# The low parts of weights split by GpSimd: a subtraction replaced by a negation on ScalarE and an accumulating DMA

## The chip, the cores and the metric

The kernel runs on one core of one Trainium2 chip. The core has TensorE (matrix products into PSUM), VectorE, ScalarE, GpSimd, a queue called SP that issues DMAs, and 16 DMA engines. The metric is the device time of one execution in microseconds. The profile shows one execution; its rows carry short names: PE is TensorE, PEld its weight load, DVE VectorE, ACT ScalarE, POOL GpSimd.

## The reference, cut to what matters

Two layers of a decoder trunk over 512 tokens of width 1024, in 32-bit floats. Each layer has a wide input projection, three token mixers (a sparse one "A", a dilated one "B", a windowed one "C"), sigmoid gates, an output projection and an MLP.

```
for l in range(DEPTH):                       # DEPTH = 2
    u = rmsnorm(h, attn_norm[l])
    (aq, ak, av, iq, ik, iw, bq, bk, bv, cq, ck, cv, gates) = split_columns(u @ w_in[l])
    ...                                      # mixers A, B, C
    g = sigmoid(gates.reshape(Bsz, L, 3, D_MODEL))
    merged = g[:,:,0]*(o_a @ w_a[l]) + g[:,:,1]*(o_b @ w_b[l]) + g[:,:,2]*(o_c @ w_c[l])
    h = h + merged @ w_o[l]
    u = rmsnorm(h, mlp_norm[l])
    h = h + square(relu(u @ w_up[l])) @ w_down[l]
return rmsnorm(h, final_norm)
```

## The kernel before, in words

TensorE multiplies in a reduced 32-bit format (`F32R`). To keep the accuracy, every operand is held as two tiles: `hi`, its rounded value, and `lo`, what the rounding left. Each product is then three matmuls (`mm3`: hi with hi, hi with lo, lo with hi).

Weights come in tiles of 128 partitions and up to 1024 columns, two steps of the inner dimension side by side. `load` issues the DMAs from SP into a `raw` tile (line 261; 6 buffers), lets ScalarE copy it into `hi` (line 264; 5 buffers), and forms `lo = raw - hi` (line 265; 5 buffers). The subtraction runs on VectorE, or, where the caller says so, on GpSimd. `load_chunk` makes the four tiles of a projection's eight inner steps; its `pool_tiles` names those of the four that GpSimd splits:

- all four tiles of each of the eight gate chunks of a layer (`gates`), 64 in all, of 768 columns;
- the last tile of the six chunks of a layer's dilated projections (`b_project`), 12 in all, of 768 columns;
- a few tiles of the index, narrow and sparse projections (`idx_project`, `small_project`, `a_project`): five of 1024 columns and two of 656.

That makes 83. The chunks of the output projection, the branches, and the MLP are split by VectorE alone.

The order of the work is set when the program is built. `merge` and `pipeline` interleave attention, gates and projections in program order; a scheduler then gives each engine, at each step, the earliest piece of work that by its reckoning is ready. Only in the first stretch is the order of SP, ScalarE and VectorE written by hand. On the chip each engine runs its queue strictly in order, and each wait holds what stands behind it. A projection of 128 tokens runs eight inner steps in one PSUM bank, the last tile of a chunk being needed from the seventh step on. After it, its result is turned on VectorE (`rope`, lines 321 to 329) and transposed on TensorE (line 337).

Of the kernel before, what the change touches and what calls it, by code (L numbers as in the profile page):

```python
# [20 lines left out]
ALU = mybir.AluOpType  # L21
# [19 lines left out]
def f32(ap):  # L41
    return ap.bitcast(F32)

class Trunk:
# [211 lines left out]
    def load(self, parts, width, lo_eng=None):  # L256

        nc = self.nc
        raw = self.st([P, 1024], "raw")
        for dst, src in parts:  # L260
            nc.sync.dma_start(dst(raw), src)
        hi = self.st([P, 1024], "hi", F32R)
        lo = self.st([P, 1024], "lo", F32R)
        nc.scalar.copy(hi[:, :width], raw[:, :width])  # L264
        (lo_eng or nc.vector).tensor_tensor(lo[:, :width], raw[:, :width], f32(hi[:, :width]), op=ALU.subtract)  # L265
        return hi, lo

    def load_chunk(self, w, k0, nk, cols, pool_tiles=()):
# [878 lines left out]
def build(tr):  # L1147
# [7 lines left out]
    with tr.tc.manual_schedule(engines={ET.SP, ET.Activation, ET.DVE}):  # L1155
# [16 lines left out]
        next(steps[1])  # L1172
        angle(2)
        wk = load(0, (0,))
        xload(2)
        next(steps[1])
        angle(1)
        next(steps[1])
        wk += load(2)
        xload(3)  # L1180
        next(steps[2])
        wk += load(4, (0,))
        next(steps[2])
        next(steps[3])
# [118 lines left out]
```

## Time and profile before

| | |
|---|---|
| median of 3 runs | 1762.99 us (1761.1 to 1763.85) |
| profiled execution, its time | 1759.4 us |
| span of its instructions | 1757.7 us |
| TensorE busy | 1690.6 us, 96% |
| VectorE busy | 1273.6 us, 72% |
| ScalarE busy | 917.7 us, 52% |
| GpSimd busy | 187.3 us, 11% |
| subtractions to lo on GpSimd | 83, 158.8 us |

Busy time is the union of an engine's instructions. It says how full an engine is, and not yet whether it sets the end. What a stretch waits for is read from the idle time ahead of TensorE's instructions and from what released them.

### The profile page before, as it was taken

How to read it: one execution, taken by the hardware profiler on the slowest of the kernel's cores; microseconds unless marked ns; L12 is line 12 of the kernel's file. 1: busy time of each engine (PE TensorE's matmuls, PEld its weight loads, DVE VectorE, ACT ScalarE, POOL GpSimd, SP SyncE). 2: the span in 40 equal slices, each digit the busy share in tenths (PEclk: the TensorE clock that was granted, in tenths of full speed). 3: DMA queues.
4: the chain of work that ended last, by engine and by line, in shares of the span. 5: the costliest groups of instructions: out<-in, count | busy, mean ns of one | idle time of the engine just before them, and what ended most of it. 6: DMA issues, size and time to landing. Idle time of an engine off the chain costs nothing.

```text
span 1757.7 us, 24534 instructions
## 1 busy us (share of the span) xinstructions
PE 1690.6 (96%) x8640; PEld 1429.0 (81%) x8640; DVE 1273.6 (72%) x2560; ACT 917.7 (52%) x1861; POOL 187.3 (11%) x163
## 2 busy tenths in 40 slices
PE   7989999999989999999999999999999999999997
PEld 5779899777779888888887798988777798888886
DVE  7986858766855868685988757596677568585858
ACT  5575645537423645454545856465473255445454
POOL 3310211221000000000012113021110000000000
PEclk9999999999999999999999999999999999999999
DMA  6224343332663142423343243433236523232412
GB/s 198 67 74 130 79 109 81 106 77 81 205 210 97 61 132 86 142 89 104 108 118 72 61 132 90 117 98 82 63 115 215 204 81 100 96 116 76 144 48 72
DMA packets 202908, 190.54 MB, mean 108 GB/s; under 512 B 17824, under 2 KB 159136, under 8 KB 202784
## 3 DMA queue, kind: packets, MB, share of 16 engines
q1 hardware_dynamic: 202784, 188.97, 36.3%
q8 instruction: 68, 1.11, 0.3%
q14 instruction: 56, 0.46, 0.1%
HBM read 167.91 MB, written 18.87 MB: 106 GB/s over the span
## 4 chain that ended last, share of the span: by engine, by line
PE 74%; DVE 16%; ACT 3%; DMA 3%; issue 3%; POOL 1%; SPq 0%; POOLq 0%; DVEq 0%; ACTq 0%
PE psg L288 19%; PE psg L290 19%; PE psg L289 18%; DMA sg<-sgd 2%; PE psl L288 2%; PE psl L289 2%; PE psl L290 2%; DVE a L682 1%; PE pst L290 1%; PE pst L289 1%; PE pst L288 1%; PE pst L337 1%; DVE t L325 1%; PE psl L369 1%; DVE lo L926 1%
## 5 line engine op out<-in xcount | busy, mean ns | idle before, releaser
L288 PE MATMUL psg<-uT,hi 128*128 128x512 f32 (+1 forms) x896 | 346.7, 387 | 0.0
L290 PE MATMUL psg<-uT,lo 128*128 128x512 f32 (+1 forms) x896 | 344.5, 384 | 0.0
L289 PE MATMUL psg<-uT,hi 128*128 128x512 f32 (+1 forms) x896 | 344.3, 384 | 0.0
L264 ACT CAST hi<-raw 128x768 fp32r<-128x768 f32 (+4 forms) x256 | 228.9, 899 | 154.9 <-PE psg L289 68.8
L265 DVE TENSOR_TENSOR lo<-raw,hi 128x1024 fp32r<-128x1024 f32 (+4 forms) x173 | 190.6, 1105 | 58.4 <-ACT hi L264 56.9
L289 PE MATMUL psg<-lo,uT 128*128 128x384 f32 (+2 forms) x624 | 218.8, 351 | 3.5 <-DVE lo L265 2.4
L265 POOL TENSOR_TENSOR lo<-raw,hi 128x768 fp32r<-128x768 f32 (+2 forms) x83 | 158.8, 1926 | 584.5 <-ACT hi L264 549.9
L288 PE MATMUL psg<-hi,uT 128*128 128x384 f32 (+2 forms) x624 | 220.6, 355 | 0.2 <-ACT uT L240 0.2
L290 PE MATMUL psg<-hi,uT 128*128 128x384 f32 (+2 forms) x624 | 218.6, 350 | 0.0
L290 PEld LDWEIGHTS psg<-uT,lo 128*128 128x128 f32 x896 | 168.8, 188 | 31.0
L289 PEld LDWEIGHTS psg<-uT,hi 128*128 128x128 f32 x896 | 169.1, 189 | 29.2 <-issue 0.7
L288 PEld LDWEIGHTS psg<-uT,hi 128*128 128x128 f32 x896 | 169.0, 189 | 29.1 <-issue 0.7
L289 PEld LDWEIGHTS psg<-lo,uT 128*128 128x128 f32 x624 | 117.7, 189 | 11.7 <-DVE lo L265 3.4
L925 ACT CAST hi<-raw 128x1024 fp32r<-128x1024 f32 x80 | 84.2, 1052 | 81.5 <-DVE raw L1000 34.3
L288 PEld LDWEIGHTS psg<-hi,uT 128*128 128x128 f32 x624 | 117.7, 189 | 7.2 <-ACT uT L240 0.6
L290 PEld LDWEIGHTS psg<-hi,uT 128*128 128x128 f32 x624 | 117.5, 188 | 6.7
L208 POOL TENSOR_TENSOR st<-st,mhalf 128x1 f32<-128x1 f32 x20 | 16.2, 811 | 946.3 <-DVE st L206 941.9
L926 DVE TENSOR_TENSOR lo<-raw,hi 128x1024 fp32r<-128x1024 f32 x80 | 96.0, 1218 | 25.4 <-ACT hi L925 25.4
L288 PE MATMUL psg<-hi,a 128*128 128x512 f32 x288 | 112.7, 391 | 0.2
L956 DVE TENSOR_TENSOR a<-t,a 128x512 fp32r<-128x512 f32 (+1 forms) x128 | 78.9, 620 | 46.9 <-ACT a L955 45.3
L290 PE MATMUL psg<-hi,a 128*128 128x512 f32 x288 | 112.4, 390 | 0.0
L289 PE MATMUL psg<-lo,a 128*128 128x512 f32 x288 | 112.1, 389 | 0.0
(230 smaller groups left out, 3348.2 us busy)
## 6 DMA issues: line engine op xcount, KB each, us to landing
raw<-in_w_in_dram SPq DMA_DIRECT2D x336, 128.0 KB, 2.8
raw<-in_w_up_dram SPq DMA_DIRECT2D x128, 256.0 KB, 3.8
raw<-in_w_down_dram SPq DMA_DIRECT2D x48, 512.0 KB, 4.9
raw<-in_w_in_dram SPq DMA_DIRECT2D x24, 512.0 KB, 3.7
sgd<-sg SPq DMA_DIRECT2D x48, 256.0 KB, 2.6
sg<-sgd SPq DMA_DIRECT2D x48, 256.0 KB, 3.9
raw<-in_w_o_dram SPq DMA_DIRECT2D x16, 512.0 KB, 3.8
a<-in_w_down_dram SPq DMA_DIRECT2D x16, 512.0 KB, 4.3
```

The costliest lines, as they stand in the source:

```text
L264: nc.scalar.copy(hi[:, :width], raw[:, :width])
L265: (lo_eng or nc.vector).tensor_tensor(lo[:, :width], raw[:, :width], f32(hi[:, :width]), op=ALU.subtract)
L288: nc.tensor.matmul(out, lh, rh, start=start, stop=False, **kw)
L289: nc.tensor.matmul(out, lh, rl, start=False, stop=False, **kw)
L290: nc.tensor.matmul(out, ll, rh, start=False, stop=stop, **kw)
L325: self.last_dve = nc.vector.tensor_tensor(v1, v1, v2, op=ALU.add)
L337: self.nc.tensor.transpose(ps[:, i, :], src[:, i * P : (i + 1) * P], self.ident)
L369: nc.tensor.matmul(out, q, k[:, 0, c0 : c0 + n], start=True, stop=False)
L682: nc.vector.tensor_tensor(lo[at], x[own], f32(dst[own]), op=ALU.subtract)
L925: nc.scalar.copy(hi, x)
L926: nc.vector.tensor_tensor(lo, x, f32(hi), op=ALU.subtract)
L956: v.tensor_tensor(lo, x, f32(hi), op=ALU.subtract)
```

## The change

Where GpSimd was given the split, ScalarE now writes `lo = -hi` after its copy to `hi`, and GpSimd's queue issues a DMA that adds the raw tile to `lo` in place. Where VectorE makes the split, all stays as it was.

```
         nc.scalar.copy(hi[:, :width], raw[:, :width])
-        (lo_eng or nc.vector).tensor_tensor(lo[:, :width], raw[:, :width], f32(hi[:, :width]), op=ALU.subtract)
+        if lo_eng is None:
+            nc.vector.tensor_tensor(lo[:, :width], raw[:, :width], f32(hi[:, :width]), op=ALU.subtract)
+        else:
+            nc.scalar.mul(lo[:, :width], f32(hi[:, :width]), -1.0)
+            lo_eng.dma_start(lo[:, :width], raw[:, :width], accum_op=ALU.add)
         return hi, lo
```

## Rows read from the trace of the kernel before

**Rows 1.** The page's busy times: us, share of the span, instructions.

```profile
PE 1690.6 (96%) x8640; PEld 1429.0 (81%) x8640; DVE 1273.6 (72%) x2560; ACT 917.7 (52%) x1861; POOL 187.3 (11%) x163
```

**Rows 2.** The chain that ended last: shares of the span by engine.

```profile
PE 74%; DVE 16%; ACT 3%; DMA 3%; issue 3%; POOL 1%; SPq 0%; POOLq 0%; DVEq 0%; ACTq 0%
```

**Rows 3.** Groups by form: busy us, mean ns of one, then idle time before.

```profile
L265 POOL TENSOR_TENSOR lo<-raw,hi 128x768 fp32r<-128x768 f32 x76 | 142.9, 1894 | 515.2 <-ACT hi L264 480.5 <-DMA raw<-in_w_in_dram 16.6 <-DVE a L682 11.6
...
L264 ACT CAST hi<-raw 128x1024 fp32r<-128x1024 f32 x104 | 109.3, 1051 | 86.8 <-PE psl L290 27.0 <-PE psg L289 22.0 <-DMA raw<-in_w_up_dram 14.8
L264 ACT CAST hi<-raw 128x768 fp32r<-128x768 f32 x112 | 92.3, 835 | 19.6 <-PE psg L290 7.0 <-PE psg L289 6.8 <-ACT a L672 2.3
```

**Rows 4.** Waits of TensorE and ScalarE: us in total, times, longest.

```profile
PE pst L337 <- DVE t L325: 13.5, 10, 3.3
...
PE pst L337 <- DVE t L219: 10.8, 2, 9.0
PE pst L757 <- ACT a L750: 3.3, 6, 0.7
...
PE psg L289 <- DVE lo L265: 2.4, 2, 1.2
...
PE pst L337 <- DVE st L197: 1.6, 1, 1.6
PE pst L337 <- DVE t L526: 1.6, 2, 0.8
...
ACT hi L264 <- DMA raw<-in_w_in_dram: 4.8, 3, 3.9
```

**Rows 5.** Order of time, VectorE and GpSimd: start us, us, what, count.

```profile
81.35 7.08 DVE L493 SCALAR_TENSOR_TENSOR a<-t,iw,a 128x384 f32<-128x384 f32 x4
...
91.09 0.61 DVE L493 SCALAR_TENSOR_TENSOR a<-t,iw,a 128x384 f32<-128x384 f32 x1
...
81.92 8.17 POOL L265 TENSOR_TENSOR lo<-raw,hi 128x768 fp32r<-128x768 f32 x4 [18.01 <-ACT hi L264]
```

**Rows 6.** Busy times from 88 to 95 us, granted clock, DMA share, GB/s.

```profile
88.00:95.00 7.00, 3.69 (x18) 3.48 (x18) 6.83 (x13) 2.86 (x7) 2.09 (x2) 0.76 0.64 142
```

**Rows 7.** Order of time, first and last of 12 dilated chunks: split, first use.

```profile
149.62 1.85 POOL L265 TENSOR_TENSOR lo<-raw,hi 128x768 fp32r<-128x768 f32 x1 [27.47 <-ACT hi L264]
...
153.36 0.33 PE L289 MATMUL psg<-lo,uT 128*128 128x384 f32 x1
...
1155.09 1.84 POOL L265 TENSOR_TENSOR lo<-raw,hi 128x768 fp32r<-128x768 f32 x1 [16.59 <-ACT hi L264]
...
1159.42 0.34 PE L289 MATMUL psg<-lo,uT 128*128 128x384 f32 x1
```

**Rows 8.** Order of time, TensorE: transposes in a new chunk's first block.

```profile
188.10 0.52 PE L337 MATMUL pst<-ident,t 128*128 128x128 f32 x3 [0.96 <-DVE t L325]
```

**Rows 9.** Order of time, first gate behind the dilated projections.

```profile
200.35 0.84 ACT L264 CAST hi<-raw 128x768 fp32r<-128x768 f32 x1 [0.58 <-ACT a L672]
...
209.30 0.39 PE L290 MATMUL psg<-uT,lo 128*128 128x512 f32 x1
```

**Rows 10.** Order of time, start: first split by GpSimd and its first use.

```profile
10.65 2.36 POOL L265 TENSOR_TENSOR lo<-raw,hi 128x1024 fp32r<-128x1024 f32 x1 [1.59 <-ACT hi L264]
...
13.07 0.79 PE L289 MATMUL psg<-lo,uT 128*128 128x512 f32 x1 [1.17 <-POOL lo L265]
```

**Rows 11.** Order of time, sparse projection, last tile: split and first use.

```profile
359.53 4.23 POOL L265 TENSOR_TENSOR lo<-raw,hi 128x1024 fp32r<-128x1024 f32 x2 [23.16 <-ACT hi L264]
...
362.79 0.39 PE L289 MATMUL psg<-lo,uT 128*128 128x512 f32 x1
```

**Rows 12.** DMA issues: count, KB each, median us from issue to landing.

```profile
raw<-in_w_up_dram SPq DMA_DIRECT2D x128, 256.0 KB, 3.8
...
a<-t SPq DMA_DIRECT2D x16, 128.0 KB, 2.9
...
raw<-in_w_down_dram SPq DMA_DIRECT2D x48, 512.0 KB, 4.9
```

## What was predicted, before the change was run

> **What bounds the kernel now.** I read the page's busy times first: TensorE is at work for 1690.6 of 1757.7 us, 96% [rows 1]. The chain of work that ended last agrees: TensorE holds 74% of it, VectorE 16%, ScalarE 3%, GpSimd 1% [rows 2]. So nothing is won by GpSimd being quicker in itself. A change can only act on the 67 us in which TensorE stands still, or add to them. What the reader should look for is therefore who ends TensorE's waits, and how long before TensorE wants it each low part is there.
>
> The groups by form price the operations: GpSimd's subtraction takes 1.89 us for a tile of 768 columns (76 times); five more tiles have 1024 columns (2.36 us [rows 10]) and two 656. ScalarE's copy from raw to hi takes 0.84 and 1.05 us for the same tiles [rows 3]. The list of TensorE's waits is led by VectorE [rows 4]. One stretch shows why: four updates by L493 take 7.08 us together, while the next one takes 0.61 [rows 5]. GpSimd is subtracting four tiles just then. The instructions that are stretched in this way, beside GpSimd's subtraction alone, read on-chip memory only (L493, L325, L219, L265, a copy in L526). Only what TensorE waits for counts.
>
> **What goes.** The 83 GpSimd subtractions go, and with them the blocking. Of TensorE's waits, L325 ends 13.5 us; two of these, of 1.0 us each, had no blocked instruction ahead (one is shown, 0.96 us [rows 8]), which leaves 11.6. L219 ends 10.8, of which 9.0 is the start of the program, so 1.8. L197 ends 1.6 (behind a blocked L219), L526 1.6, and VectorE's own split L265 2.4 [rows 4]. That is 19.0 us. The longest of these waits, 3.31 us, is followed by a stretch of 7 us with a mean granted clock of 0.76, about 3.4 us at 1.2 GHz in place of 2.4, which lost 1.7 us [rows 6]. Together 20.7; a blocked instruction is not always the whole of the wait behind it, so I take **20 us back**. The bounds are 0 (descriptor writing by GpSimd blocks as much as its reading did) and 21.
>
> **What ScalarE gets.** A negation reads and writes tiles of the same form as the copy ahead of it, so it costs the same: 76 x 0.84 + 5 x 1.05 + 2 x 0.72 (the last by its columns) = 71 us more, 52% to 56% of the span. Behind each stands whatever is queued on ScalarE: casts of projected queries and keys, exponentials, the next hi. TensorE waits for ScalarE directly very little (exponentials: 3.3 us in 6 waits [rows 4]), and VectorE, which waits for it, is idle 28% of the time. ScalarE's 3% of the chain, and a little of VectorE's 16% that stands behind ScalarE, make 7% of 71: **+5 us**. Bounds 0 and 71.
>
> **What the accumulating DMA costs.** Its landing L, from the end of the negation until lo may be read, stands in place of the subtraction. No row shows such a DMA. The nearest are: on-chip to on-chip, 128 KB, 2.9 us; weight loads of 256 KB 3.8 and of 512 KB 4.9 [rows 12]. The tile has 384 KB. As a plain copy between the tiles of on-chip memory that is about 3.0, the low end. An accumulation reads 768 KB; the two loads rise by 1.1 us per 256 KB, so 6.0 is the high end. I take the middle, **L = 4.5**, as the sources are on chip, but twice the bytes are read and the weight loads share the engines.
>
> The Trainium skill, "DMA: Bandwidth & Descriptors", section on the anatomy of one DMA on the GpSimd path, gives a fit of 2.0 us plus bytes over 436e3, which would be 2.9 us here (an estimate by that page); my sum would then come to -10. "Collectives: The Full Stack", on the bandwidth ceiling, says that a reducing transfer needs two source reads and runs at half the rate; by both pages an estimate is 3.8 us, and the sum comes to -2. No row here shows either.
>
> Against the subtraction, lo of a 768-column tile comes later by 0.84 + L - 1.84 = L - 1.0, that is 3.5 us. Where that is more than the slack, TensorE waits:
>
> - Last tile of each of 12 chunks of the dilated projections: in the first chunk GpSimd is done at 151.47 and the first product that needs the tile starts at 153.36, slack 1.9; in the last chunk the slack is 2.5 [rows 7]. The twelve have 1.3 to 2.5, mean 1.77, so they come L - 2.77 = 1.7 late, 21 us in all. The schedule can put other ready work there: three transposes of the block before already stand in the middle of a new chunk, behind five of its eight steps [rows 8]. I count half: **10.4**.
> - The first gate behind a pair of dilated projections (4 times): hi starts at 200.35, and more copies follow. Copy and negation three times are 5.0 us, with 0.5 for casts between; the third lo lands at 205.9 + 4.5 = 210.4, and is wanted at 209.30 [rows 9]. 4 x 1.1 = **4.4**.
> - Start: GpSimd began at 10.65, when hi was done; negation to 11.7, landing at 16.2; wanted at 13.07 already [rows 10]. **3.1**.
> - Projection of the sparse attention, 1024 columns: begun at 359.53, done 2.36 later at 361.9, wanted at 362.79 [rows 11]. Later by 1.05 + 4.5 - 2.36 = 3.2, so 2.3 too late, in both layers: **4.6**.
> - The other tiles have 2.4 us or more, most of them 4 to 30; what lateness is left there is under 1 us each, taken as nothing.
>
> GpSimd's queue holds little behind the DMA: powers of one column, most of them far from these tiles. SP's loads wait longer for a raw tile to come free, since the DMA reads it last. That costs nothing: a weight tile's landing ended a wait of ScalarE's copy only 3 times, 4.8 us, from the projection weights [rows 4]. If this cover were gone, each of the 83 would be late by the same 3.5 us.
>
> Sum: 10.4 + 4.4 + 3.1 + 4.6 = 22.5 late, + 5 on ScalarE, - 20 given back = **+8 us**. The profiled execution took 1759.4 us (a span of 1757.7 and 1.7 around it), so 1767; the median of the runs is 3.6 above it, so **1771**. A measurement of this kernel tells about 0.2%, 3.5 us, from no change.
>
> **Rivals.**
> - *Short landing, faster.* At L = 3.0 the chunks lose 2, the gates 0, the start 1.6, the sparse projection 1.6: 5.2 + 5 - 20 = -10, 1753. It decides from L below about 3.9 on. For it: the 2.9 of the on-chip copy [rows 12]. Against: that one is a third of the size and reads once. By the fit of "DMA: Bandwidth & Descriptors" this is the case that would come.
> - *Cancelling, no change.* With L near 3.9 the two sides meet and the time stays at 1763. For it: 3.8 us, the row of 256 KB [rows 12]. Against: the two sides have nothing to do with each other, and the band is only 0.5 us of L wide. By the half rate of "Collectives: The Full Stack" this one would come.
> - *Long landing that nothing fills.* L = 6.0 and no other work in the gaps: 39 + 10.4 + 4.6 + 7.6 = 62, + 5 - 20 = +47, 1810. For it: TensorE's order is fixed, and a wait of 1.2 us for VectorE's split, twice, stands unfilled today [rows 4]. Against: the transposes of rows 8.
> - *No relief, or ScalarE on the path.* If GpSimd's descriptor work blocks VectorE as its reads did, +28, 1791; if a third of the 71 us lands on the path, some +27, 1790. For it: VectorE waits for ScalarE in many places. Against: ScalarE has 44% left.
>
> **How the numbers follow.** Forecast, slower by 4 to 25 us (1767 to 1788): 0.37. Short landing: 0.30. Cancelling: 0.13. Long and unfilled: 0.14. No relief or ScalarE: 0.06. So faster 0.30, same 0.13, slower 0.57. The range goes from a little beyond the short landing to the long one, 1751 to 1808; signs differ within it, so the forecast's own range stands above.
>
> **What would show it.** Right: L493, L325 and L219 at their unblocked 0.6 to 0.75 us everywhere; no subtraction on GpSimd; a new ScalarE group of 83 at 0.8 to 1.05 us; a median landing of 4 to 5 us; TensorE's waits now ended by the DMA into lo, about 20 us in all, at the last tile of the chunks above all. Wrong: a landing under 3.9 with waits gone (faster), or waits for lo of 3 us and more, perhaps with the clock falling to 1.2 GHz behind them, as it did behind the 3.31 us wait (slower than the range).

## The result, and the profile after

The kernel became slower by 3.1%: a median of 1815.12 us (1814.39 to 1822.07, 4 runs) beside 1762.05 us for the kernel before on the same chip, ratio 1.031 with an interval of 1.0282 to 1.0337. That is 53 us where +8 was forecast, 7 us above the top of the range. The sign was right, the size was not.

The page's busy times of the kernel after, to be set beside [rows 1]:

```profile
span 1812.7 us, 24736 instructions
...
PE 1709.8 (94%) x8640; PEld 1438.8 (79%) x8640; DVE 1239.8 (68%) x2560; ACT 978.8 (54%) x1944; POOL 100.7 (6%) x163
```

The span grew by 55.0 us. TensorE does the same 8640 products, so there are only two places for it: TensorE's time without work went from 67.1 us (1757.7 less 1690.6) to 102.9, which is +35.8, and its busy time rose by 19.2. Two thirds of the loss are waiting, one third is the same work done more slowly.

The chain that ended last, shares of the span by engine, answers to [rows 2]:

```profile
PE 60%; issue 14%; DMA 11%; DVE 8%; ACT 5%; SPq 0%; POOL 0%; POOLq 0%; ACTq 0%; DVEq 0%
```

VectorE's share went from 16% to 8%, and the DMAs' from 3% to 11%. The fall of TensorE's share to 60% is not to be read as idleness: the chain here runs back through GpSimd's issues, and seven pieces of "issue" ahead of such issues, of 18 to 24 us each, make 149 us, in which TensorE is busy for 140. Who ends the waits is in the waits of TensorE, in total, times and longest, to be set beside [rows 4]:

```profile
PE psg L293 <- DMA lo<-raw: 42.7, 17, 6.9
PE psg L294 <- DMA lo<-raw: 19.0, 14, 2.7
PE psg L292 <- DVE sg L895: 10.0, 9, 3.6
PE pst L341 <- DVE t L219: 9.0, 1, 9.0
PE pst L341 <- DVE t L329: 2.3, 4, 0.9
```

The diff moved the lines below it down by four (L289 is L293, L290 is L294, L325 is L329, L337 is L341). The waits for `rope` fell from 13.5 us to 2.3 and VectorE's split no longer ends one in L293: the relief came. (Not all of that fall need be relief. Where TensorE does not stand for `lo`, in e3 below, the waits for `rope` are 9.8 us and those for VectorE's split 2.0; some of them may be over here because TensorE comes later.) The accumulating DMA now ends 31 waits of 61.7 us together, where the prediction counted 22.5. L293 multiplies the projections' weights, L294 the gates'.

That VectorE is free shows in the order of time at the place of [rows 5], the same four updates of 384 columns:

```profile
84.88 2.72 DVE L497 SCALAR_TENSOR_TENSOR a<-t,iw,a 128x384 f32<-128x384 f32 x4
```

They took 7.08 us beside GpSimd's subtraction, and 2.72 now, though GpSimd issued one of its DMAs in the midst of them, from 86.19 to 87.06 us. So this issue did not block them. The Trainium skill, "SBUF — State Buffer", section "Who interferes with whom", has it that a VectorE instruction with two inputs in on-chip memory contends with GpSimd where GpSimd reads that memory, and not where it only writes. The trace agrees with the first half (7.08 us beside a subtraction, which reads); that an issue only writes is shown by no run.

The new operations, groups by form (busy us, mean ns of one, idle before), ScalarE's two and GpSimd's one:

```profile
L268 ACT ACTIVATE lo<-hi 128x768 fp32r<-128x768 f32 x76 | 64.0, 845 | 1.4
L268 ACT ACTIVATE lo<-hi 128x1024 fp32r<-128x1024 f32 x5 | 5.3, 1056 | 0.1
...
L269 POOL DMA_DIRECT2D lo<-raw x83 | 71.8, 869 | 730.1 <-ACT lo L268 281.7 <-DMA raw<-in_w_in_dram 175.9 <-DVE m L513 47.8
```

And the landings, KB each and median us from issue to landing:

```profile
raw<-in_w_up_dram SPq DMA_DIRECT2D x128, 256.0 KB, 3.9
lo<-raw POOLq DMA_DIRECT2D x76, 384.0 KB, 4.8
...
lo<-raw POOLq DMA_DIRECT2D x5, 512.0 KB, 6.7
```

The negation costs what the copy costs, 0.85 us. The landing of 384 KB was taken at 4.5 and is 4.8 in the median; the weight loads that priced it [rows 12] are where they were.

One dilated chunk in the order of time (ScalarE's negation, GpSimd's issue, TensorE's wait), the one of [rows 7]:

```profile
148.46 0.85 ACT L268 ACTIVATE lo<-hi 128x768 fp32r<-128x768 f32 x1
...
149.60 0.86 POOL L269 DMA_DIRECT2D lo<-raw  x1 [22.81 <-ACT lo L268]
...
152.12 0.34 PE L292 MATMUL psg<-hi,uT 128*128 128x384 f32 x1
155.23 0.44 PE L293 MATMUL psg<-lo,uT 128*128 128x384 f32 x1 [2.77 <-DMA lo<-raw]
```

From the end of the negation (149.31) to the first product with `lo` 5.92 us pass. TensorE does the six steps whose tiles are there and the first product of the seventh, and then nothing for 2.77 us: no transpose and no product of another chunk steps in. In eight of the twelve chunks it is so; in the other four the three transposes of [rows 8] stand ahead of the wait, and 1.0 to 2.3 us of waiting are left. Read in this way, the twelve chunks have 4.2 to 6.1 us from negation to use, 5.05 in the mean, and each of them waits, 1.04 to 2.86 us, 23.8 together. The other long waits are 6.87 at the start, 3.84 at the index projection of the second layer, 3.51 and 3.35 at the sparse projections. The start, the gate behind the dilated projections and the first sparse projection in the order of time, to be set beside [rows 9 to 11]:

```profile
10.61 1.06 ACT L268 ACTIVATE lo<-hi 128x1024 fp32r<-128x1024 f32 x1
...
19.86 0.79 PE L293 MATMUL psg<-lo,uT 128*128 128x512 f32 x1 [6.87 <-DMA lo<-raw]
...
213.97 1.58 ACT L268 ACTIVATE lo<-hi 128x768 fp32r<-128x768 f32 x2
...
220.65 0.50 PE L294 MATMUL psg<-uT,lo 128*128 128x512 f32 x1 [2.68 <-DMA lo<-raw]
...
383.78 1.06 ACT L268 ACTIVATE lo<-hi 128x1024 fp32r<-128x1024 f32 x1
...
390.77 0.50 PE L293 MATMUL psg<-lo,uT 128*128 128x512 f32 x1 [3.51 <-DMA lo<-raw]
```

From negation to use these are 8.2, 5.8 (the gate's is the first of the two negations, over at 214.82) and 5.9 us.

The rest is clock. Busy times by stretch (PE, PEld, DVE, ACT, POOL, then granted clock, DMA share, GB/s), three of ten stretches at 1.2 GHz in place of 2.4:

```profile
156.40:159.80 3.40, 3.40 (x12) 3.40 (x12) 0.29 (x1) 0.64 (x2) 0.00 (x0) 0.50 0.60 153
...
391.90:395.30 3.40, 3.40 (x10) 2.62 (x9) 2.14 (x5) 0.21 (x1) 0.00 (x0) 0.50 0.86 199
...
1282.80:1289.60 6.80, 5.55 (x13) 4.40 (x14) 2.14 (x5) 0.21 (x1) 0.00 (x0) 0.50 0.84 184
sum 37.40, PE 35.58 PEld 31.05 DVE 16.74 ACT 8.49 POOL 1.42; mean PE 3.56 PEld 3.10 DVE 1.67 ACT 0.85 POOL 0.14
```

All ten begin during or within 2 us behind a wait for `lo` of 1.85 to 3.84 us. Three waits of 2.2 to 2.8 us (at 1049.6, 1070.1 and 1182.9) have none behind them, so not every wait is followed by one. TensorE is busy for 35.6 us in them, half of which, 17.8, is lost. The kernel before had two such stretches with 9.1 us of work, 4.6 lost. That is 13.2 of the 19.2 us by which busy time rose; where the other 6.0 come from is open.

### The profile page after: what moved, and what is told of

It is laid out like the page before. It is cut to its first block, busy times and chain, and to the rows that moved or that the text cites. A ratio compares the mean times of both kernels' runs of the same rounds, so it can differ in the third digit from the quotient of the medians.

```text
span 1812.7 us, 24736 instructions
## 1 busy us (share of the span) xinstructions
PE 1709.8 (94%) x8640; PEld 1438.8 (79%) x8640; DVE 1239.8 (68%) x2560; ACT 978.8 (54%) x1944; POOL 100.7 (6%) x163
## 4 chain that ended last, share of the span: by engine, by line
PE 60%; issue 14%; DMA 11%; DVE 8%; ACT 5%; SPq 0%; POOL 0%; POOLq 0%; ACTq 0%; DVEq 0%
PE psg L293 16%; PE psg L294 15%; PE psg L292 15%; DMA lo<-raw 7%; DMA sg<-sgd 2%; PE psl L293 2%; PE psl L294 2%; PE psl L292 2%; DMA raw<-in_w_in_dram 2%; ACT hi L264 1%; PE pst L341 1%; PE pst L293 1%; PE pst L294 1%; PE pst L292 1%; ACT a L390 1%
## 5 line engine op out<-in xcount | busy, mean ns | idle before, releaser
L294 PE MATMUL psg<-uT,lo 128*128 128x512 f32 (+1 forms) x896 | 347.6, 388 | 19.1 <-DMA lo<-raw 19.0
L293 PE MATMUL psg<-uT,hi 128*128 128x512 f32 (+1 forms) x896 | 345.3, 385 | 0.0
L264 ACT CAST hi<-raw 128x768 fp32r<-128x768 f32 (+4 forms) x256 | 229.3, 898 | 141.3 <-PE psg L293 63.3
L293 PE MATMUL psg<-lo,uT 128*128 128x384 f32 (+2 forms) x624 | 226.5, 363 | 42.7 <-DMA lo<-raw 42.7
L292 PE MATMUL psg<-hi,uT 128*128 128x384 f32 (+2 forms) x624 | 224.2, 363 | 1.5 <-ACT uT L240 1.2
L294 PE MATMUL psg<-hi,uT 128*128 128x384 f32 (+2 forms) x624 | 224.2, 360 | 0.0
L266 DVE TENSOR_TENSOR lo<-raw,hi 128x1024 fp32r<-128x1024 f32 (+4 forms) x173 | 183.5, 1064 | 58.5 <-ACT hi L264 55.7
L294 PEld LDWEIGHTS psg<-uT,lo 128*128 128x128 f32 x896 | 169.2, 189 | 57.0 <-DMA lo<-raw 26.2
L293 PEld LDWEIGHTS psg<-uT,hi 128*128 128x128 f32 x896 | 169.6, 189 | 29.4 <-issue 0.7
L293 PEld LDWEIGHTS psg<-lo,uT 128*128 128x128 f32 x624 | 121.5, 195 | 56.2 <-DMA lo<-raw 48.4
L292 PEld LDWEIGHTS psg<-hi,uT 128*128 128x128 f32 x624 | 121.1, 194 | 9.5 <-ACT uT L240 1.6
L294 PEld LDWEIGHTS psg<-hi,uT 128*128 128x128 f32 x624 | 121.8, 195 | 7.4 <-DVE uT L241 0.4
L269 POOL DMA_DIRECT2D lo<-raw x83 | 71.8, 869 | 730.1 <-ACT lo L268 281.7
L294 PE MATMUL psg<-hi,a 128*128 128x512 f32 x288 | 112.3, 390 | 0.0
L293 PE MATMUL psg<-lo,a 128*128 128x512 f32 x288 | 112.1, 389 | 0.0
L411 DVE TENSOR_TENSOR a<-pst,a 128x384 fp32r<-128x384 f32 (+1 forms) x100 | 60.4, 623 | 70.2 <-ACT a L410 69.6
```

Source lines behind the costliest of these rows:

```text
L266: nc.vector.tensor_tensor(lo[:, :width], raw[:, :width], f32(hi[:, :width]), op=ALU.subtract)
L269: lo_eng.dma_start(lo[:, :width], raw[:, :width], accum_op=ALU.add)
L292: nc.tensor.matmul(out, lh, rh, start=start, stop=False, **kw)
L293: nc.tensor.matmul(out, lh, rl, start=False, stop=False, **kw)
L294: nc.tensor.matmul(out, ll, rh, start=False, stop=stop, **kw)
L411: self.last_dve = nc.vector.tensor_tensor(pt[:, 1, :n], ps, f32(pt[:, 0, :n]), op=ALU.subtract)
```

## The experiments

Theory, formed on this profile: the relief is as large as forecast or larger; the loss is lateness of `lo` at a few places in TensorE's fixed order, which nothing fills, plus the clock behind these waits. Rivals: the DMAs cost by their traffic whoever reads them; ScalarE's 71 us are on the path; the 64 gate transfers crowd the queue and so make the others late. All ratios are to the kernel before on the same chip, with their intervals.

| kernel | median us (runs) | ratio | TensorE's waits for the DMA into lo |
|---|---|---|---|
| changed kernel | 1815.12 (4) | 1.031 [1.0282, 1.0337] | 61.7 us, 31 |
| e2: no low part made | 1726.13 (4) | 0.983 [0.9813, 0.9847] | none |
| e1: negation alone | 1737.15 (4) | 0.9883 [0.9866, 0.9901] | none |
| e3: low part made, not read | 1749.32 (5) | 0.9955 [0.9939, 0.997] | none |
| e4: DMA for gates, GpSimd for projections | 1762.0 (10) | 1.0025 [1.0015, 1.0035] | 19.5, 15 |
| e5: DMA for projections, GpSimd for gates | 1817.11 (4) | 1.0333 [1.0314, 1.0351] | 45.9, 17 |
| e12: DMA for 12 dilated tiles, VectorE for the rest | 1781.65 (4) | 1.014 [1.0118, 1.0162] | 25.5, 12 |
| e13: DMA for gates, VectorE for the rest | 1761.45 (10) | 1.0023 [1.0009, 1.0037] | 18.6, 15 |
| e9: plain copy in place of the accumulation | 1778.19 (4) | 1.0118 [1.0093, 1.0143] | 30.7, 21 |
| e7: first tile of a chunk in place of the last | 1779.47 (4) | 1.0123 [1.0102, 1.0144] | 30.6, 18 |
| e10: DMA for first tiles alone, VectorE for the rest | 1760.47 (10) | 1.001 [1.0001, 1.0019] | 2.6, 1 |
| e6: VectorE for all 83 | 1744.87 (4) | 0.9927 [0.9907, 0.9946] | none |
| e11: e6, and 83 copies off the core | 1748.15 (5) | 0.9947 [0.9932, 0.9962] | none |

One reservation holds for all but e9: the scheduler that writes the engines' queues answers to each edit with another order on TensorE, VectorE and ScalarE. Of TensorE's 8640 products, e3 has another one than the changed kernel in 310 places and e1 in 94; e9 has the same on all three engines. A difference of well under 1% between two of these kernels may be that order.

### What each part of the change costs: e2, e1, e3

e2 makes no low part at the 83 places (against the kernel before):

```diff
-        lo = self.st([P, 1024], "lo", F32R)
+        lo = None if lo_eng is not None else self.st([P, 1024], "lo", F32R)
...
-        (lo_eng or nc.vector).tensor_tensor(lo[:, :width], raw[:, :width], f32(hi[:, :width]), op=ALU.subtract)
+        if lo_eng is None:
+            nc.vector.tensor_tensor(lo[:, :width], raw[:, :width], f32(hi[:, :width]), op=ALU.subtract)
+        else:
+            return hi, hi
```

> Where GpSimd had the split, lo is not made at all and hi is used in its place (values not the reference's): no negation, no DMA, no subtraction for 83 tiles. Theory: 1736 to 1746, within 5 us of the negation-only kernel, since ScalarE's negations cost little. Rival A: 30 us or more below the negation-only kernel.

e1 leaves the DMA out:

```diff
             nc.scalar.mul(lo[:, :width], f32(hi[:, :width]), -1.0)
-            lo_eng.dma_start(lo[:, :width], raw[:, :width], accum_op=ALU.add)
```

> The accumulating DMA is left out, the negation stays: lo holds -hi, so the values are not the reference's. Theory (lateness: TensorE waits for the landing of the accumulating DMA, and its clock falls behind those waits; ScalarE's added work is cheap and the end of GpSimd's reads gives some 20 us back): 1740 to 1750, no TensorE wait for a DMA into lo, no clock drops beyond the two of before. Rival A (ScalarE's 61 us more busy time lies on the path): 1775 or more. Rival B (the extra DMA traffic slows weights): like the theory, 1740 to 1750.

e3 makes the low part in full and multiplies with the high part in its place:

```diff
             lo_eng.dma_start(lo[:, :width], raw[:, :width], accum_op=ALU.add)
+            return hi, hi
```

> Negation and accumulating DMA both run, but the products read hi in place of the 83 lo tiles (values not the reference's), so nothing on TensorE waits for a landing. Theory: 1742 to 1755, as the negation-only kernel within 6 us. Rival B (10% more DMA traffic is what costs): 1765 or more, with waits for raw weights.

Read as steps, with 1% of the kernel before being 17.6 us: without GpSimd's subtractions and their low parts the kernel is 1.70% faster, 30 us; the negation on ScalarE takes 0.53% of it back, 9 us; the DMA that nobody reads another 0.72%, 13 us; and reading what it writes 3.55%, 62 us. The sum is +3.1%. So most of the loss hangs on the reading; the 9 and the 13 us are of the size that another order could make. In e3 the landings are the same, 4.9 us at 384 KB, and so are ScalarE's work and GpSimd's:

```profile
PE 1690.6 (97%) x8640; PEld 1427.5 (82%) x8640; DVE 1240.6 (71%) x2560; ACT 979.5 (56%) x1944; POOL 100.1 (6%) x163
```

Its waits for `rope`:

```profile
PE pst L342 <- DVE t L330: 9.8, 8, 2.2
```

Every operation is in place here but the dependence. Beside the changed kernel TensorE's busy time is 19.2 us shorter, and its time without work is 54.6 us for 102.9, 48.3 shorter. So both the waits and the loss in busy time, the clock's with it, come with the dependence. The 61.7 us of waits for `lo` cost 48.3 us of idle time, as its other waits are shorter than in e3.

### Which tiles: e4, e5, e12, e13

e4 keeps the DMA at the 64 gate tiles (`n_pool` is the number of tiles of a chunk that were GpSimd's, 4 at the gates); e5 turns the test around:

```diff
+            if n_pool == 4:
                 nc.scalar.mul(lo[:, :width], f32(hi[:, :width]), -1.0)
                 lo_eng.dma_start(lo[:, :width], raw[:, :width], accum_op=ALU.add)
+            else:
+                lo_eng.tensor_tensor(lo[:, :width], raw[:, :width], f32(hi[:, :width]), op=ALU.subtract)
```

> Only the 64 gate tiles take the negation and the DMA; the 19 tiles of projections are subtracted by GpSimd as before. Theory: the projections' 42.7 us of waits and most clock drops (about 17 us) go, some 6 us of blocked VectorE come back: 1755 to 1775. Rivals A and B (a cost per tile): 64 of 83 parts of the 53 us stay, about 1804.

> The 19 tiles of the projections are split by ScalarE's negation and the accumulating DMA, the 64 tiles of the gates by GpSimd's subtraction, as before. Theory A (the waits at the start, the index projection, the dilated chunks and the sparse projection belong to these places and stand also without the gates'): TensorE waits for the DMA some 41 us (6.9 + 3.8 + 23.8 + 6.9), the gates' subtractions still block VectorE, so 1800 to 1815. Theory B (the landings are late because 64 more of them share the queue): waits of under 20 us and 1765 to 1785.

e4 stays within 0.25% of the kernel before, so the rivals that charge every one of the tiles alike fall. e5, with the DMA at 19 tiles only, loses 3.3%, as much as the change at all 83. Its time is 2 us above what the first theory gave, and its waits (TensorE, in total, times, longest; L296 and L344 there are L293 and L341 of the changed kernel) are 45.9 us for 41:

```profile
PE psg L296 <- DMA lo<-raw: 45.9, 17, 6.9
PE pst L344 <- DVE t L332: 11.1, 6, 3.4
```

Its landings at 384 KB are 4.9 us with less than a quarter of the transfers, so crowding by the gates is out. The second row, with 3.4 us at the longest, agrees with VectorE still being held up here, as in [rows 4] (3.3); in e1 and e3, without GpSimd's subtractions, the longest is 2.2.

Next the twelve dilated tiles by themselves (e12), and the gates without GpSimd's subtractions elsewhere (e13):

```diff
-    def gemm_tok(self, uT, w, cols, tbs, evac, wk=None, pool_tiles=(3,)):
+    def gemm_tok(self, uT, w, cols, tbs, evac, wk=None, pool_tiles=()):
...
-            yield from self.gemm_tok(uT, w, cols, range(NT), ev)
+            yield from self.gemm_tok(uT, w, cols, range(NT), ev, None, (3,))
...
-        wk = self.load_chunk(w, 0, NK, [(OFF_G + i * D + f * P, P) for i in range(3)], (0, 1, 2, 3))
+        wk = self.load_chunk(w, 0, NK, [(OFF_G + i * D + f * P, P) for i in range(3)])
...
-        wk = load(0, (0,))
+        wk = load(0)
...
-        wk += load(4, (0,))
+        wk += load(4)
```

(e13 is the same without the second and the third piece.)

> Only the 12 last tiles of the dilated chunks keep the negation and the accumulating DMA; VectorE makes the other 71 splits. The measure is the kernel in which VectorE makes all 83 (1745). Theory A (each of the 12 leaves TensorE standing, nothing fills the gap, and the clock falls behind the longer ones): waits for lo of 20 to 26 us, at least four stretches at the half clock, 1770 to 1785. Theory B, the step of the prediction that halved these waits because the schedule puts other ready work there: waits of 8 to 13 us and 1754 to 1762.

> The 64 gate tiles keep the negation and the accumulating DMA; VectorE makes the 19 projection tiles. Theory A (the loss hangs on the tiles of the projections, which are late at one place each; gate tiles are late by little): waits for lo of 10 to 20 us in many small pieces, at most three stretches at the half clock, 1752 to 1766. Theory B (the gates' 64 transfers crowd each other, and that makes the landings late): 1780 and more.

In e12 twelve tiles cost 2.13% of the kernel before against e6, 37 us in the medians and 31.9 in the two profiled executions. Its waits for the DMA and its stretches at the half clock (busy by stretch, first and sum of six):

```profile
PE psg L293 <- DMA lo<-raw: 25.5, 12, 3.3
```

```profile
151.10:157.90 6.80, 5.55 (x17) 5.55 (x18) 0.29 (x1) 0.64 (x2) 0.00 (x0) 0.50 0.59 155
...
sum 23.80, PE 22.55 PEld 21.67 DVE 12.44 ACT 5.73 POOL 0.00; mean PE 3.76 PEld 3.61 DVE 2.07 ACT 0.95 POOL 0.00
```

25.5 us of waits and half of 22.55, 11.3, make 36.8. e6 has 6.8 us at the half clock, some 3 of them lost, so this would be about 34 us more than e6. The profiled executions differ by a little less: TensorE stands 21.8 us longer than in e6 and is busy for 10.1 longer. This settles the halved term: the waits of the twelve chunks stand almost in full, and carry almost half as much again in busy time. In e13 the 64 gate tiles cost 0.96% against e6, 17 us, in 15 waits of 18.6 us:

```profile
PE psg L294 <- DMA lo<-raw: 18.6, 15, 2.1
```

Five times as many tiles lose half as much. The second theory of e13 falls.

### How late, and where in the chunk: e9, e7, e10

e9 overwrites `lo` with a plain copy:

```diff
-            lo_eng.dma_start(lo[:, :width], raw[:, :width], accum_op=ALU.add)
+            lo_eng.dma_start(lo[:, :width], raw[:, :width])
```

> As the changed kernel, with a plain copy of raw into lo from GpSimd's queue in place of the accumulation (the products then use raw as lo, so the values are not the reference's). If the second read of the accumulation makes the landing long: median landing of 384 KB at 3.0 to 3.8 us in place of 4.8, time 1785 to 1800. If queueing and GpSimd's issue make it: 4.5 or more, and about 1810.

Its landings:

```profile
lo<-raw POOLq DMA_DIRECT2D x76, 384.0 KB, 3.0
lo<-raw POOLq DMA_DIRECT2D x5, 512.0 KB, 4.4
```

And its waits:

```profile
PE psg L293 <- DMA lo<-raw: 25.2, 13, 5.6
...
PE psg L294 <- DMA lo<-raw: 5.5, 8, 1.7
```

The adding is 1.8 us of the 4.8. Without it the waits halve, five of the ten stretches at the half clock are left, and the time falls by 1.9%, somewhat more than expected. TensorE, VectorE and ScalarE have the same instructions in the same order as in the changed kernel, so only the transfers, their issue and the values differ: this is the cleanest evidence that their length sets the loss. It also shows that nothing on TensorE moves up into a gap: with half the waits the order is the same.

The rival of the short landing promised 1753 us for L = 3.0; with a median landing of 3.0 the kernel takes 1778, still 1.2% slower than before. But L was to run from the end of the negation to the first use, and at the eight dilated chunks that still wait this takes 3.0 to 5.0 us. So a landing of 3.0 in the median does not win; whether an L of 3.0 at every place would is not shown.

The Trainium skill, "DMA: Bandwidth & Descriptors", section on the anatomy of one DMA on the GpSimd path, gives 2.9 us for such a copy by its fit (an estimate); e9's 3.0 agrees. At 512 KB the same fit would give 3.2, and the five copies took 4.4 in the median. The doubled bytes by the Trainium skill's "Collectives: The Full Stack", section on the bandwidth ceiling, made 3.8 of it, and that section measures transfers between cores; the accumulating transfer measured 4.8, so here the trace decides against that estimate.

e7 gives each chunk's first tile to the DMA in place of its last, with SP, ScalarE and VectorE's order following from that:

```diff
-    def gemm_tok(self, uT, w, cols, tbs, evac, wk=None, pool_tiles=(3,)):
+    def gemm_tok(self, uT, w, cols, tbs, evac, wk=None, pool_tiles=(0,)):
```

> As the changed kernel, but in the projections the first tile of a chunk takes the negation and the DMA in place of the last; the first one finds a free buffer a whole chunk earlier. Theory (lateness): the waits at the dilated and sparse projections (some 34 us) and their clock drops (some 12 us) go; the gates' and the start's stay: 1760 to 1775. Rivals A and B (ScalarE's work, traffic): the same 83 negations and DMAs run, so about 1812 as the changed kernel.

The waits at the dilated chunks vanish; what is left are 21.0 us at the gates and 9.6 at the start and the index projection:

```profile
PE psg L294 <- DMA lo<-raw: 21.0, 16, 2.9
PE psg L293 <- DMA lo<-raw: 9.6, 2, 6.9
```

The time falls by 1.9%, and stays 4 us above the top of what was expected: six stretches at the half clock are still there. e10 goes on along that line: the gates too give only their first tile to the DMA, and the start gives none (33 tiles in all, VectorE makes the other 50).

```diff
-    def gemm_tok(self, uT, w, cols, tbs, evac, wk=None, pool_tiles=(3,)):
+    def gemm_tok(self, uT, w, cols, tbs, evac, wk=None, pool_tiles=(0,)):
...
-        wk = self.load_chunk(w, 0, NK, [(OFF_G + i * D + f * P, P) for i in range(3)], (0, 1, 2, 3))
+        wk = self.load_chunk(w, 0, NK, [(OFF_G + i * D + f * P, P) for i in range(3)], (0,))
...
-        wk = load(0, (0,))
+        wk = load(0)
...
-        wk += load(4, (0,))
+        wk += load(4)
```

> Negation and DMA for the first tile of each gate and projection chunk alone (33 tiles), VectorE splits all others, the two of the start too. Theory: no wait for a landing, GpSimd's reads gone, VectorE 50 x 0.95 = 48 us more: 1730 to 1748. Rival: if VectorE sets the end, 1755 or more; if each accumulating DMA costs by itself, above the kernel with all splits on VectorE.

This missed: 1760.5 us. The waits for `lo` are gone but for one of 2.6 us, and yet the kernel is 0.83% slower than e6, 15 us. TensorE's busy time is 3.9 us longer than in e6 (1695.0 to 1691.1); the other 11 us are the wait for `lo` and many short ones, most of them for VectorE. Which part of it is the transfers and which the other order isn't settled.

### A version that beats both: e6 and e11

e6 gives all 83 subtractions to VectorE:

```diff
-        if lo_eng is None:
+        if True:
```

> VectorE makes all splits, GpSimd none; no negation, no accumulating DMA. Theory (what GpSimd's reads cost VectorE is worth some 30 us on the path, and lo from VectorE is there early enough): 83 x 0.95 us = 79 us more on VectorE, of which little is on the path, so 1730 to 1750. Rival (VectorE is full, its chain sets the end): 1760 or more.

```profile
PE 1691.1 (97%) x8640; PEld 1428.2 (82%) x8640; DVE 1304.7 (75%) x2643; ACT 917.9 (53%) x1861; POOL 27.9 (2%) x80
```

It is 0.73% faster than the kernel before (0.54 to 0.93) and 3.7% faster than the changed one. VectorE takes 0.95 us for a tile of 768 columns, half of what GpSimd took, and no subtraction on GpSimd holds it up: its busy time is only 31 us above that of before, for 83 more instructions.

e11 adds to e6 the same 83 transfers, as plain copies of the raw tile to memory off the core:

```diff
+        if lo_eng is not None:
+            d = self.dr.tile([P, 1024], F32, name=self.uid("xd"))
+            lo_eng.dma_start(d[:, :width], raw[:, :width])
```

> VectorE makes all splits, as in the run where it made all 83 (1744.9 us), and in addition GpSimd's queue copies each of the same 83 raw tiles to memory off the core, where nobody reads them (an extra write that the reference does not have). So the transfers are there, and the raw tile is held until they have read it, but neither ScalarE nor TensorE has anything to do with them. Theory A (the 12 us by which the kernel with unread accumulations exceeds the one with the negation alone come from the transfers and from raw tiles held longer): 1754 to 1760. Theory B (they come from the other order in which the engines' queues are written when the program is built, or from ScalarE): 1743 to 1748.

The result, 1748.15, is at the upper edge of what theory B gave, and the interval of its ratio overlaps with that of e6: 83 plain transfers that nobody waits for, and raw tiles held for them, made 0.2%, which these runs cannot tell from nothing. So the 13 us of e3 over e1 are not explained by traffic of that kind. Whether they are the accumulation's double reading or the order of the queues stays open.

Deeper buffers for `hi` and `lo`, which might let the transfers start earlier, were not tried.

## Why the prediction was off

The direction came from the right mechanism: low parts that land late outweigh what is given back. The step that failed is the one that took the lateness of the twelve chunks as half filled by other work, and with it the clock behind these waits, which was in no term. In the prediction's own steps:

- **Relief, 20 us taken, bounds 0 and 21.** Right in kind: `rope` and the updates run unblocked. Too small in size, and above the upper bound: e2 gives 30 us; TensorE's waits for VectorE fall from 52.7 us to 29.4 in its trace. (In e2 nothing waits for these low parts either, and its trace has no stretch at the half clock behind the start, where the kernel before had two, with 4.6 us lost; both are in the 30.)
- **ScalarE, +5.** e1 beside e2 gives 9, a small share of the 71 us, as argued, and within what another order can make.
- **L = 4.5.** The median landing is 4.8. L was defined to the first use, though, and there it is 5.05 in the mean of the chunks, 5.9 at the sparse projection (negation over at 384.84, use at 390.77) 8.9 at the index projection of the second layer, and 8.2 at the start, where a tile of 512 KB lands among the first loads. One L for all sizes and places was too simple.
- **Chunks, 21 us halved to 10.4. This is the step that failed.** "The schedule can put other ready work there" was read from transposes that stand inside a chunk [rows 8]. They stand where the scheduler had put them, in the same four of the twelve chunks before and after, so their time was in the slacks of 1.3 to 2.5 us already, and halving for them counted it twice. Nothing more was put there when the program was built anew, and nothing moves into a gap that opens on the chip (e9). The twelve waits are 23.8 us here and 25.5 in e12, between the unhalved 21 and the 27 that 12 x (L - 2.77) makes at the measured 5.05.
- **The clock, not in the sum.** 13 us more than before are lost in stretches at 1.2 GHz. The prediction had the row for it [rows 6], used it for the relief (1.7 us) and named it among what would make the numbers wrong, but gave the twelve new waits no such term.
- **Gates, 4.4.** The waits are 19.0 us, because not only the first gate behind a pair of projections is late. Their effect on the time is smaller than this size says: 17 us in e13, ScalarE's 64 negations included, and +0.25% beside GpSimd's subtractions in e4.
- **Start 3.1, sparse 4.6, the others nothing.** Measured 6.9, 6.9 and, at the index projection of the second layer, 3.8, with 1.3 more at a tile of 656 columns. The first three are tiles of 1024 columns, 512 KB, which land in 5.4 to 7.8 us and not in 4.5.
- **The transfers themselves, nothing.** e3 beside e1 has 13 us, of which the cause is open. Raw tiles that come later are not it, as far as ScalarE's copies in L264 show: they wait 23.5 us for weights in e3 and in e1 alike.

By the steps of e2, e1 and e3 the sum is -30 + 9 + 13 + 62 = +54 us, where -20 + 5 + 22.5 was written. With the chunks left whole the written sum would have been +18; the clock, the gates, the transfers and the tiles of 512 KB make the rest, against a larger relief. The rival of the long landing that nothing fills, 1810, came nearest: it was right in "nothing fills", with a landing of 4.8 and not 6.0, and with the clock in place of the missing 1.2 us. That its number is so near is in part luck: its waits of 62 us are 39 at the chunks and 10.4 at the gates, where 23.8 and 19.0 were measured. "No relief" falls by the updates of 2.72 us and by e2. "Short landing" and "cancelling" did not come, since the landing was 4.8; that a median of 3.0 does not win either, e9 shows. (In the short landing the chunks' 2 us would be 1.4 by the prediction's own halving, which changes its sum by less than 1.)

## What to carry to other kernels

Where an engine runs its queue in order, an operand that comes 2 us late at the last step costs these 2 us each time, however many other products are ready elsewhere (e12: 25.5 us of waits in twelve chunks). Halve nothing for work that might step in unless a row shows it doing so, and see whether the slack that you read has that work in it already. Behind each such wait look at the granted clock: here a quarter of the loss, 13 of 55 us, was the same products at 1.2 GHz. Before a step on the critical operand goes to a DMA, price the path from the end of what precedes it to the first use at the tile's own size, and try the idle quarter of the next engine first: VectorE, 28% idle, took all 83 subtractions and made the kernel 0.7% faster.

## What the runs showed of the hardware

- An accumulating DMA from on-chip to on-chip memory took 4.8 us for 384 KB and 6.7 for 512 KB in the median; a plain one between the same tiles 3.0 and 4.4. Issuing an accumulating one kept GpSimd for 0.87 us, without blocking VectorE's instructions on two inputs from on-chip memory (2.72 us for four, 7.08 beside a subtraction); in the changed kernel no VectorE instruction beside one of the 83 issues took over 0.1 us longer than its like.
- Waits of 1.9 to 3.8 us had 3.4 us at 1.2 GHz behind them ten times in one execution (6.8 us once), and some waits of the same length had none.
